# A two-layer block on one core: the loop over further rounds moved ahead of the experts, and the last expert's rows added by one-hot products

## The chip, the cores and the metric

The kernel runs on one core of one Trainium2 chip. A core has five engines with an instruction queue each, worked off in order: TensorE (PE; its weight loads are listed as PEld), VectorE (DVE), ScalarE (ACT), GpSimd (POOL) and SyncE (SP, which here only issues DMAs). The metric is the device time of one execution in microseconds (us), from the first to the last instruction and what lies around them.

## The reference

Two transformer blocks over 1024 rows of width 1024. The change concerns the end of the second one, the mixture of experts, and the last norm:

```python
expert_idx = (g_sel[:, None] * EXPERTS_PER_GROUP + top_i).reshape(-1)   # 2 of 32 experts per row
order = jnp.argsort(expert_idx)
counts = jnp.bincount(expert_idx, length=N_EXPERTS)
...
def expert_block(args):                      # 128 rows of one expert
    xb, e = args
    hb = jax.nn.silu(xb @ w_g[e]) * (xb @ w_u[e])     # 1024 -> 512
    return hb @ w_d[e]                                # 512 -> 1024
...
y = y_pad[dest] * gates[order][:, None]
out = jnp.zeros((t, d), xt.dtype).at[token_idx[order]].add(y)
...
x = x + out
return rms_norm_2(x, norm_final)
```

## The kernel before

All of the work up to the experts (attention layers, norms, the router) is untouched. Then `route` (L1358 on) works out which rows go to which expert, and two products (`table`, L1462) write `idt`: for each of the 32 experts a list of up to 128 row numbers to read (column 0) and up to 128 places in `y_d` to write (column 1; `y_d` in HBM has two rows for each row of x, one for each of its two experts). `rounds_t` says how many further rounds of 128 rows the fullest expert needs.

**The experts.** The work is cut into 192 units (L1536 to 1541): for each expert e two halves of the gate weights (g), two of the up weights (u) and, one expert later, two of the down weights (d). So the order is g(e) g(e) u(e) u(e) d(e-1) d(e-1), and at the very end d(31) d(31). A unit is 1 MB of weights: SP loads it (`eraw`), ACT writes its rounded copy (`ehi`), DVE the remainder (`elo`; POOL does it for the second u unit of each expert, L1579), and PE runs 12 products of 512 columns over it, in threes (`mm3`, L131): high by high, high by low, low by high. Splits run two units ahead of PE (`AHEAD`), with three buffers of `ehi` and `elo`. The ring of loaded weights has 6 slots (11 for the first 150 units). The code is in `tc.manual_schedule()`: every engine runs its instructions in the order in which the loop at L1590 writes them.

**Rows in and out.** `gather` (L1492) is an indirect DMA from POOL's queue that reads an expert's 128 rows into `xe`. PE transposes them (`x_part`). After the second d unit of an expert, `scatter` (L1529) copies the two PSUM banks `yo` to `ys` on ACT, and POOL issues an indirect DMA that writes the 128 rows to their places in `y_d`. Each such write waits for the one before it, since both write `y_d`.

**The further rounds.** Behind the experts stands a loop (L1652) over `rounds`, and in it one over the 32 experts (L1653), that does the same work for rows beyond the first 128. `rounds` is read into a register of every engine at L1651. With these inputs it is zero: the trace has no instruction of the inner loop, but all engines pass the read and the branch.

**The end.** For each of 8 tiles of 128 rows (L1684): load both y rows of every row (`fy`, 1 MB), two DVE instructions that scale and add them to the rows of x (`x3t`, loaded from L1638), a square with sum on ACT, the reciprocal root on POOL (`rsq`, L199), and the final scaling: for even tiles ACT by the root and POOL by the norm's weights, for odd tiles one DVE instruction. Then the tile goes out.

Of the kernel before, what the change touches and what calls it, by code (L numbers as in the profile page):

```python
# [27 lines left out]
def block_kernel(  # L28
# [1505 lines left out]


    units = []  # L1536
    for e in range(NE + 1):
        if e < NE:
            units += [(nm, e, half) for nm in "gu" for half in range(2)]
        if e:  # L1540
            units += [("d", e - 1, half) for half in range(2)]
# [29 lines left out]
    for i in range(len(wide)):  # L1571
        if i not in raws:
            load_unit(i)
    AHEAD = HB - 1
    parts, banks, hbs, hss, tps, xss, yos = {}, {}, {}, {}, {}, {}, {}

    def split_unit(i):
        nm, e, half = units[i]
        parts[i] = esplit(raws.pop(i), pool if (nm, half) == ("u", 1) else dve)  # L1579

    with tc.manual_schedule():
        for e in range(2):
# [7 lines left out]
        for i, (nm, e, half) in enumerate(units):  # L1590
# [44 lines left out]
    x3t = []
    for i in range(4):
        xt = er2.tile([128, 2048], F32, name="x3t", tag="eraw2", bufs=RAWB2)
        sp.dma_start(out=xt.rearrange("p (a n) -> p a n", a=2),  # L1638
                     in_=x3_d[i * 256:(i + 1) * 256, :].rearrange("(a p) n -> p a n", p=128))
        x3t += [xt[:, 0:D], xt[:, D:]]  # L1640
    nfw = er2.tile([128, 2048], F32, name="nfw", tag="eraw2", bufs=RAWB2)[:, 0:D]
    sp.dma_start(out=nfw, in_=norm_final_2.partition_broadcast(128))


    shift = mo.tile([128, 1], F32, name="shift")
    pool.memset(shift, float(C))

    rounds_e = ew.tile([128, D], I32, name="rounds_e", tag="ys", bufs=2)
    dve.tensor_copy(out=rounds_e[:, 0:1], in_=rounds_t)
    with tc.tile_critical():  # L1650
        rounds = nc.values_load(rounds_e[0:1, 0:1], min_val=0, max_val=7)  # L1651
    with tc.For_i(0, rounds) as r_:  # L1652
        with tc.For_i(0, NE) as e_:  # L1653
            pos = ew.tile([128, 16], F32, name="pos", tag="pos", bufs=1)
            TS(pos, posk, shift, SUB)
            ti = ew.tile([128, 2], I32, name="ti", tag="ti", bufs=1)
            table(pos, lambda j: tkr[:, j], 2, ti)
            gather(xes[0], ti[:, 0:1])
            xs = x_tile()
            for g in range(2):  # L1660
                x_part(xes[0], xs, g)
            gu = []
            for w in (w_e_gate_2, w_e_up_2):
                o = bank("gu", 4)
                for half in range(2):
                    up_half(o, xs, esplit(eload(w[bass.ds(e_, 1), half].rearrange("o p n -> (o p) n")), dve), half)
                gu.append(o)
            hb = ew.tile([128, 512], F32, name="hb", tag="hb", bufs=2)
            A(hb, gu[0], AF.Silu)
            TT(hb, hb, gu[1], MUL)  # L1670
            tp = bank("tpe", 2)
            h_part(tp, hb)
            hs = h_tile()
            split(*hs, tp.rearrange("p (k n) -> p k n", k=4))
            yo = y_bank()
            for half in range(2):
                down_half(yo, hs, esplit(eload(w_e_down_2[bass.ds(e_, 1), half].rearrange("o p n -> (o p) n")), dve),
                          half)
            scatter(yo, ti[:, 1:2])
            TS(shift, shift, 1024.0, ADD)  # L1680
        TS(shift, shift, float(C - NE * 1024), ADD)


    for t in range(8):  # L1684
        rs = slice(t * 128, (t + 1) * 128)
        xt = x3t[t]
        yt = er.tile([128, 2 * D], F32, name="fy", tag="eraw", bufs=RAWB)
        sp.dma_start(out=yt, in_=y_d.rearrange("(t k) d -> t (k d)", k=2)[rs, :])
        STT(xt, yt[:, 0:D], pk[:, 0, t:t + 1], xt, MUL, ADD)
        STT(xt, yt[:, D:], pk[:, 1, t:t + 1], xt, MUL, ADD)  # L1690
        r = rstd_of(xt, D, junk_tile())
        if t % 2 == 0:
            A(xt, xt, AF.Copy, scale=r)
            TT(xt, xt, nfw, MUL, eng=pool)
        else:
            STT(xt, xt, r, nfw, MUL, MUL)
        sp.dma_start(out=out[0, rs, :], in_=xt)
# [35 lines left out]
```

## Time and profile before

| | |
|---|---|
| Device time, median of 3 runs | 2148.75 us (2148.54 to 2151.77) |
| Device time of the profiled execution | 2150.52 us |
| Its span, first to last instruction | 2148.8 us |
| Share of the span busy: PE, PEld, DVE, ACT, POOL | 91%, 77%, 67%, 55%, 29% |
| HBM read, written | 356.35 MB, 39.85 MB |

The shares are means over stages that differ. The experts run from about 1471 us to 2089 us; what follows up to 2148.8 us is the loop that is passed and the end. Rows of the profile give a start and a duration, the engine (a small q stands for its instruction sequencer or DMA queue), the line, the operation, out<-in by the names of the program, and in brackets the idle time before and what ended it.

### The profile page before, as it was taken

To read this page: it belongs to the slowest core of one execution; us is meant where nothing else is said; L and a number is where in the kernel's file an instruction comes from. 1 tells how busy PE (TensorE), PEld (TensorE's weight loads), DVE (VectorE), ACT (ScalarE), POOL (GpSimd) and SP (SyncE) were. 2 spreads that over 40 slices of the span, in tenths; PEclk is the share of its full clock that TensorE was granted. 3 is DMA by queue.
4 is the path that set the end of the run, shared out by engine and by line. 5 is a ranking of instruction groups with operands and counts; after the bars stand their busy time and mean duration, and the time that the engine had idled before them with its cause. 6 is when DMAs were issued, how large, how long until landed. Compare 5 with 4: busy or idle time off the path is not lost.

```text
span 2148.8 us, 32901 instructions
## 1 busy us (share of the span) xinstructions
PE 1961.3 (91%) x12914; PEld 1653.1 (77%) x12914; DVE 1446.0 (67%) x1923; ACT 1177.3 (55%) x1868; POOL 632.5 (29%) x522
## 2 busy tenths in 40 slices
PE   3999899999999999999999999995999999999980
PEld 2878796887777988889887997894777777777760
DVE  6476774656687754686557855746777777877765
ACT  3454553445465533564335634643777777777752
POOL 3362110144453000241004300003444444344425
PEclk8999999999997999999999999996999999999995
DMA  9212334621111263212622156464999999999956
GB/s 295 70 50 57 111 90 137 193 78 40 31 40 30 60 191 90 64 45 85 191 59 59 51 161 205 157 245 178 347 366 361 379 355 357 358 360 354 360 202 240
DMA packets 218934, 381.60 MB, mean 178 GB/s; under 512 B 50165, under 2 KB 173077, under 8 KB 193177
## 3 DMA queue, kind: packets, MB, share of 16 engines
q1 hardware_dynamic: 194520, 345.79, 46.9%
q10 hardware_dynamic: 15040, 16.89, 2.3%
q0 software_dynamic: 9216, 16.80, 2.1%
q8 instruction: 102, 1.67, 0.3%
q14 instruction: 56, 0.45, 0.1%
HBM read 356.35 MB, written 39.85 MB: 184 GB/s over the span
## 4 chain that ended last, share of the span: by engine, by line
PE 51%; issue 25%; POOL 9%; DVE 7%; DMA 6%; ACT 3%; POOLq 0%; ACTq 0%; SPq 0%; DVEq 0%; another core or an unknown queue 0%
PE mm L133 11%; PE mm L134 11%; PE mm L135 11%; POOL xe L1493 3%; PE tp L189 3%; POOL y_d L1532 2%; PE z L741 1%; DMA xp<-u_d 1%; PE sc L1139 1%; PE sc L1168 1%; PE at L599 1%; PE at L601 1%; PE os L770 1%; DVE wlo L43 1%; DVE kp L43 1%
## 5 line engine op out<-in xcount | busy, mean ns | idle before, releaser
L43 DVE TENSOR_TENSOR elo<-eraw,ehi 128x2048 fp32r<-128x2048 f32 x160 | 402.0, 2528 | 131.2 <-ACT ehi L40 131.2
L40 ACT ACTIVATE ehi<-eraw 128x2048 fp32r<-128x2048 f32 x192 | 366.9, 1912 | 18.8 <-PE yo L135 12.6
L133 PE MATMUL mm<-whi,fs 128*128 128x256 f32 x1152 | 335.4, 293 | 0.9 <-ACT whi L40 0.9
L134 PE MATMUL mm<-wlo,fs 128*128 128x256 f32 x1152 | 334.4, 291 | 0.8 <-DVE wlo L43 0.8
L135 PE MATMUL mm<-whi,fs 128*128 128x256 f32 x1152 | 331.1, 289 | 0.0
L43 DVE TENSOR_TENSOR wlo<-raw,whi 128x1024 fp32r<-128x1024 f32 x156 | 198.6, 1273 | 148.3 <-ACT whi L40 146.7
L40 ACT ACTIVATE whi<-raw 128x1024 fp32r<-128x1024 f32 x156 | 164.8, 1056 | 214.8 <-PE mm L134 93.9
L133 PEld LDWEIGHTS mm<-whi,fs 128*128 128x128 f32 x1152 | 225.0, 196 | 9.0 <-issue 5.5
L134 PEld LDWEIGHTS mm<-wlo,fs 128*128 128x128 f32 x1152 | 225.6, 196 | 8.1 <-issue 6.0
L135 PEld LDWEIGHTS mm<-whi,fs 128*128 128x128 f32 x1152 | 224.2, 195 | 2.4 <-issue 2.3
L134 PE MATMUL gu<-elo,xh 128*128 128x512 f32 x512 | 207.1, 405 | 15.9 <-POOL elo L43 14.4
L133 PE MATMUL gu<-ehi,xh 128*128 128x512 f32 x512 | 208.0, 406 | 2.5 <-ACT ehi L40 2.5
L133 PE MATMUL mm<-fs,whi 128*128 128x512 f32 x480 | 197.2, 414 | 7.5 <-DVE mst L43 4.1
L135 PE MATMUL gu<-ehi,xl 128*128 128x512 f32 x512 | 202.9, 396 | 0.0
L134 PE MATMUL mm<-fs,whi 128*128 128x512 f32 x480 | 197.0, 410 | 1.2 <-DVE fs L52 1.2
L135 PE MATMUL mm<-fs,wlo 128*128 128x512 f32 x480 | 195.1, 406 | 0.0
L43 POOL TENSOR_TENSOR elo<-eraw,ehi 128x2048 fp32r<-128x2048 f32 x32 | 147.6, 4612 | 97.2 <-ACT ehi L40 97.2
L134 PEld LDWEIGHTS gu<-elo,xh 128*128 128x128 f32 x512 | 96.6, 189 | 47.1 <-POOL elo L43 24.6
L133 PEld LDWEIGHTS mm<-fs,whi 128*128 128x128 f32 x480 | 94.0, 196 | 39.4 <-issue 9.6
L133 PEld LDWEIGHTS gu<-ehi,xh 128*128 128x128 f32 x512 | 96.7, 189 | 23.8 <-ACT ehi L40 2.9
L135 PEld LDWEIGHTS gu<-ehi,xl 128*128 128x128 f32 x512 | 96.5, 189 | 21.5
L135 PEld LDWEIGHTS mm<-fs,wlo 128*128 128x128 f32 x480 | 94.2, 196 | 23.4 <-issue 4.0
(467 smaller groups left out, 4234.5 us busy)
## 6 DMA issues: line engine op xcount, KB each, us to landing
eraw<-in_w_e_up_dram SPq DMA_DIRECT2D x64, 1024.0 KB, 7.1
eraw<-in_w_e_down_dram SPq DMA_DIRECT2D x64, 1024.0 KB, 7.3
eraw<-in_w_e_gate_dram SPq DMA_DIRECT2D x64, 1024.0 KB, 7.6
raw<-in_w_in_dram SPq DMA_DIRECT2D x92, 512.0 KB, 3.8
raw<-in_w_out_dram SPq DMA_DIRECT2D x32, 512.0 KB, 3.5
wa<-in_w_ada_dram SPq DMA_DIRECT2D x16, 512.0 KB, 5.9
fy<-y_d SPq DMA_DIRECT2D x8, 1024.0 KB, 8.7
xt<-in_x_dram SPq DMA_DIRECT2D x8, 512.0 KB, 5.6
```

Of the source, the lines that this page charges most:

```text
L40: act.activation(out=o, in_=i, func=f, **kw)
L43: (eng or dve).tensor_tensor(out=o, in0=a, in1=b, op=op)
L133: pe.matmul(out=o, lhsT=l[0], rhs=r[0], start=start, stop=False)
L134: pe.matmul(out=o, lhsT=l[0], rhs=r[1], start=False, stop=False)
L135: pe.matmul(out=o, lhsT=l[1], rhs=r[0], start=False, stop=stop)
L189: pe.transpose(o[0:s.shape[-1], j * 128:j * 128 + s.shape[0]], s, ident[0:s.shape[0], 0:s.shape[0]])
L599: pe.matmul(out=ov[:, hh, ch], lhsT=full[:, hh, ch], rhs=v(ch, hh), start=True, stop=s0 is None)
L601: pe.matmul(out=ov[:, hh, ch], lhsT=qs[r, ch * 128:(ch + 1) * 128], rhs=s0[r], start=False, stop=True)
L741: pe.matmul(out=zp[:, 0:w], lhsT=qc[r, pr, t * 128:(t + 1) * 128], rhs=kc_full[r, pr, s0 * 128:s0 * 128 + w], start=True, stop=True)
L770: pe.matmul(out=os_[:, hd * 64:hd * 64 + 64], lhsT=pt[:, j * 128:(j + 1) * 128], rhs=vc_full[:, s0 + j, hd * 64:hd * 64 + 64], start=(hd = ...
L1493: pool.indirect_dma_start(out=xe, out_offset=None, in_=xn_d[:, :], in_offset=bass.IndirectOffsetOnAxis(ap=itok, axis=0), bounds_check=S - ...
L1532: pool.indirect_dma_start(out=y_d[:, :], out_offset=bass.IndirectOffsetOnAxis(ap=irow, axis=0), in_=ys, in_offset=None, bounds_check=2 * S ...
```

## The change

Five edits. The loop over further rounds, with its read of `rounds`, now stands between the routing and the experts. The last expert's second g unit and its two u units come after the down units of expert 30, so that the order ends g(31) d(30) d(30) g(31) u(31) u(31) d(31) d(31). Expert 31 writes nothing to `y_d`: its places are written with zeros right after expert 0's rows, and its own rows are multiplied into place from SBUF with one-hot matrices that `last_places` prepares behind d(26). The loads of x and of the norm's weights are issued behind d(27), those of the y rows behind d(30). And the end is spread over ACT (scaling of the second y row), POOL (adding it), PE, DVE and ACT again.

```diff
     def scatter(yo, irow):
...
+        put(ys, irow)
+
+    def put(ys, irow):
         pool.indirect_dma_start(out=y_d[:, :], out_offset=bass.IndirectOffsetOnAxis(ap=irow, axis=0),
                                 in_=ys, in_offset=None, bounds_check=2 * S - 1, oob_is_err=False)
...
+        new = [(nm, e, half) for nm in "gu" for half in range(2)] if e < NE else []
+        old = [("d", e - 1, half) for half in range(2)] if e else []
+        units += new[0:1] + old + new[1:] if e == NE - 1 else new + old
...
+    for e in range(2):
+        gather(xes[e], idt[:, e, 0:1])
...
+    with tc.tile_critical():
+        rounds = nc.values_load(rounds_t[0:1, 0:1], min_val=0, max_val=7)
+    with tc.For_i(0, rounds) as r_:
+        with tc.For_i(0, NE) as e_:
...
+    def last_places():
+        d_ = mo.tile([128, 2, 8], F32, name="d_")
+        TS(d_, posk.rearrange("p (i t) -> p i t", i=2), -1024.0 * (NE - 1), ADD)
+        g_ = mo.tile([128, 2, 8], F32, name="g_")
+        TS(g_, d_, 0.0, ALU.is_ge)
+        TT(g_, g_, pk, MUL)
+        TT(pkl, g_[:, 0], g_[:, 1], ADD)
+        TT(d_[:, 0], d_[:, 0], d_[:, 1], MAX)
+        m = ew.tile([128, 8, 128], F32, name="lm", tag="ys", bufs=2)
+        TT(m, islot[:, None].to_broadcast([128, 8, 128]), d_[:, 0, :, None].to_broadcast([128, 8, 128]), ALU.is_equal)
+        for g in range(2):
+            tp = bank("tpe", 2)
+            transpose4(tp, [m[:, 4 * g + i] for i in range(4)])
+            A(onehot[:, 4 * g:4 * g + 4], tp.rearrange("p (k n) -> p k n", k=4), AF.Copy)
...
+    def first_sum(t):
+        yt, xt = yts[t], x3t[t]
+        A(yt[:, D:], yt[:, D:], AF.Copy, scale=pk[:, 1, t:t + 1])
+        STT(xt, yt[:, 0:D], pk[:, 0, t:t + 1], xt, MUL, ADD)
+        TT(xt, xt, yt[:, D:], ADD, eng=pool)
+        if len(yts) < 8:
+            row_of_y()
+
+    def last_sum(t, ys):
+        xt = x3t[t]
+        for n in range(2):
+            o = bank("gu", 4)
+            for i, p_ in enumerate(ys):
+                pe.matmul(out=o, lhsT=onehot[:, t], rhs=p_[:, n * 512:n * 512 + 512], start=(i == 0), stop=(i == 1))
+            STT(xt[:, n * 512:n * 512 + 512], o, pkl[:, t:t + 1], xt[:, n * 512:n * 512 + 512], MUL, ADD)
+        A(junk_tile(), xt, AF.Square, scale=float(D) ** -0.5, accum_out=ssf[:, t:t + 1])
+
+    def last_norm(t0, t1):
+        rsq(ssf[:, t0:t1], ssf[:, t0:t1], t1 - t0)
+        for t in range(t0, t1):
+            STT(x3t[t], x3t[t], ssf[:, t:t + 1], nfw_[0], MUL, MUL)
+            sp.dma_start(out=out[0, t * 128:(t + 1) * 128, :], in_=x3t[t])
...
-                if half:
+                if half and e < NE - 1:
                     scatter(yos.pop(e), idt[:, e, 1:2])
+                    if e == 0:
+                        zt = ew.tile([128, D], F32, name="zt", tag="ys", bufs=2)
+                        pool.memset(zt, 0.0)
+                        put(zt, idt[:, NE - 1, 1:2])
+                    if e == NE - 6:
+                        last_places()
+                    if e == NE - 5:
+                        rest_of_stream()
+                    if e == NE - 2:
+                        rows_of_y()
...
+        ys = [ew.tile([128, 2048], F32R, name="e" + p_, tag="e" + p_, bufs=HB)[:, 0:D] for p_ in ("hi", "lo")]
+        yo = yos.pop(NE - 1).rearrange("p a n -> p (a n)")
+        for t in range(2):
+            first_sum(t)
+        split(*ys, yo)
+        for t in range(2, 4):
+            first_sum(t)
+        for t in range(4):
+            last_sum(t, ys)
+            first_sum(4 + t)
+        last_norm(0, 4)
+        for t in range(4, 8):
+            last_sum(t, ys)
+            if t % 2:
+                last_norm(t - 1, t + 1)
```

`rest_of_stream` issues the four loads of `x3t` (1 MB each) and that of the norm's weights (0.5 MB), `rows_of_y` the first six loads of `fy`; the other two follow when a slot comes free.

Three places in the order of instructions matter below. The first is ACT between the routing and the experts. `idt` is the table that the first gather reads. Before, it is followed at once by the copies of the first expert's rows:

```order
L40 ACTIVATE gd<-gd 128x32 [waits DVE_49]
L40 ACTIVATE d<-d 128x8 [waits DVE_49]
L40 ACTIVATE idt<-gu,twos 128x64 [waits PE_49,Pool_49]
L40 ACTIVATE xh<-tpe 128x512 [waits PE_49] x2
L40 ACTIVATE ehi<-eraw 128x2048 [waits DMAHW1_49,Activation_49]
```

Now it stands behind the read of `rounds` (L1593) and in front of the branch past the loop (L1594), with a wait for SP that was not there:

```order
L40 ACTIVATE gd<-gd 128x32 [waits DVE_49]
L40 ACTIVATE d<-d 128x8 [waits DVE_49]
L1808 UNCONDITIONAL_BRANCH [waits DMAHW2_49,DMAHW1_49,DMAHW3_49,DMAHW0_49,DMAHW4_49,SP_sequencer_49,DMAHW5_49,DVE_49,DMAHW6_49,PE_49,DMAHW7_49,Activation_49,Pool_49]
L1593 TENSOR_LOAD rounds_t
L1592 UNCONDITIONAL_BRANCH
L40 ACTIVATE idt<-gu,twos 128x64 [waits SP_49,PE_49,Pool_49]
L1594 COMPARE_AND_BRANCH
```

The read and the branch have moved in between. The second place is POOL around expert 0's write to `y_d` (`y_d<-ys`). DMASWn is the semaphore of POOL's n-th DMA lane of eight, taken in turn. Before:

```order
L1493 DMA xe_14940<-xn_d,idt 128x1024 [waits DMASW1_49,PE_49]
L43 TENSOR_TENSOR elo<-eraw_14858,ehi 128x2048 [waits DMAHW4_49,Activation_49]
L1493 DMA xe_14939<-xn_d,idt 128x1024 [waits DMASW2_49,PE_49]
L1532 DMA y_d<-ys,idt 2048x1024 [waits Activation_49]
L43 TENSOR_TENSOR elo<-eraw,ehi 128x2048 [waits DMAHW4_49,Activation_49]
```

Now the zeros (`zt`) and their write stand between it and POOL's next split:

```order
L43 TENSOR_TENSOR elo<-eraw_14858,ehi 128x2048 [waits Activation_49]
L1493 DMA xe_14939<-xn_d,idt 128x1024 [waits DMASW4_49,PE_49]
L1535 DMA y_d<-ys,idt 2048x1024 [waits Activation_49]
L1750 MEMSET zt 128x1024
L1535 DMA y_d<-zt,idt 2048x1024 [waits DMASW7_49,Pool_49]
L43 TENSOR_TENSOR elo<-eraw,ehi 128x2048 [waits DMAHW2_49,Activation_49]
L1493 DMA xe_14940<-xn_d,idt 128x1024 [waits DMASW5_49,PE_49]
```

The new write has a wait on lane 7. The third place is DVE behind the second d unit of expert 26. Before, one remainder follows the other:

```order
L43 TENSOR_TENSOR xl_19014<-tpe_19041,xh_19013 128x512 [waits Activation_49]
L43 TENSOR_TENSOR elo_19054<-eraw_18974,ehi_19053 128x2048 [waits DMAHW2_49,Activation_49]
L43 TENSOR_TENSOR elo_19073<-eraw_18994,ehi_19072 128x2048 [waits DMAHW3_49,Activation_49]
L43 TENSOR_TENSOR elo_19096<-eraw_19022,ehi_19095 128x2048 [waits DMAHW4_49,PE_49,Activation_49]
L43 TENSOR_TENSOR hl_19118<-tpe_19106,hh_19117 128x512 [waits Activation_49]
```

Now the six instructions of `last_places` stand between the second and the third; `lm` is what PE transposes:

```order
L43 TENSOR_TENSOR elo_19280<-eraw_19200,ehi_19279 128x2048 [waits DMAHW3_49,Activation_49]
L43 TENSOR_TENSOR elo_19299<-eraw_19220,ehi_19298 128x2048 [waits DMAHW4_49,Activation_49]
L47 TENSOR_SCALAR d__19319<-posk_14841 128x16
L47 TENSOR_SCALAR g__19321<-d__19319 128x16 [waits DVE_49]
L43 TENSOR_TENSOR g__19321<-g__19321,pk_14842 128x16 [waits DVE_49]
L43 TENSOR_TENSOR pkl_15230<-g__19321 128x8 [waits DVE_49]
L43 TENSOR_TENSOR d__19319<-d__19319 128x8
L43 TENSOR_TENSOR lm_19326<-islot_14844,d__19319 128x1024 [waits DMASW6_49,DMASW7_49,DMASW2_49,DVE_49]
L43 TENSOR_TENSOR elo_19343<-eraw_19248,ehi_19342 128x2048 [waits DMAHW5_49,PE_49,Activation_49]
```

On PE the eight transposes of `lm` follow directly on the last product of d(26), ahead of the next g unit.

## Rows read from the trace of the kernel before

**Rows 1.** Busy us per engine (instructions) in stretches; then PE clock, DMA share, GB/s
```profile
1560.00:1700.00 140.00, 136.52 (x626) 108.95 (x625) 109.21 (x67) 105.05 (x82) 60.68 (x22) 1.00 0.96 366
2089.30:2148.80 59.50, 0.00 (x0) 0.00 (x0) 31.08 (x20) 14.33 (x21) 28.06 (x21) 0.53 0.55 217
```

**Rows 2.** Chain that ended last, 2088 to 2112 us: start, us, what
```profile
2089.25 1.03 ACT ys L40
...
2091.39 5.22 POOLq L1650
...
2097.49 3.43 DMA y_d<-ys,idt
...
2101.72 4.80 DMA fy<-y_d
```

**Rows 3.** Timeline of the end: start, us, engine, line, operation, form [idle before]
```profile
2114.12 3.36 DVE L52 SCALAR_TENSOR_TENSOR x3t<-fy,pk,x3t 128x1024 f32<-128x1024 f32 x1
...
2140.34 1.04 ACT L40 ACTIVATE junk<-x3t 128x1024 bf16<-128x1024 f32 x1
2140.51 2.34 POOL L43 TENSOR_TENSOR x3t<-x3t,nfw 128x1024 f32<-128x1024 f32 x1 [1.26 <-ACT x3t L40]
...
2143.85 1.28 DVE L52 SCALAR_TENSOR_TENSOR x3t<-x3t,rstd,nfw 128x1024 f32<-128x1024 f32 x1 [5.01 <-POOL rstd L43]
```

**Rows 4.** Timeline between routing and experts: the table's last products, the first gather
```profile
1468.67 1.68 PE L1470 MATMUL gu<-rr,mt__14954 128*128 128x64 f32 x7
...
1471.65 1.31 POOL L1493 DMA_INDIRECT xe<-xn_d,idt  x1 [9.01 <-issue]
```

**Rows 5.** L1729, POOL's drains: count, shortest/median/longest ns, first and last start
```profile
L1729 POOLq DRAIN  x3: 51/110/769, 2143.2 to 2148.5; - x3
```

**Rows 6.** Timeline behind expert 0's last unit: POOL, DVE, PE
```profile
1518.38 1.16 POOL L1532 DMA_INDIRECT y_d<-ys,idt  x1 [4.45 <-ACT ys L40]
...
1522.14 0.68 DVE L43 TENSOR_TENSOR hl<-tpe,hh 128x512 fp32r<-128x512 f32 x1
1522.32 4.62 POOL L43 TENSOR_TENSOR elo<-eraw,ehi 128x2048 fp32r<-128x2048 f32 x1 [2.78 <-ACT ehi L40]
...
1526.99 0.50 PE L134 MATMUL gu<-elo,xh 128*128 128x512 f32 x1 [0.43 <-POOL elo L43]
```

**Rows 7.** DMA issues, 1518 to 1519 us: queue, operation, us from issue to landing
```profile
y_d<-ys,idt POOLq DMA_INDIRECT x1, 8.1
```

**Rows 8.** Timeline behind d(26): DVE, ACT, PE
```profile
2003.79 4.48 DVE L43 TENSOR_TENSOR elo<-eraw,ehi 128x2048 fp32r<-128x2048 f32 x2
...
2006.70 1.03 ACT L40 ACTIVATE ys<-yo 128x1024 f32<-128x1024 f32 x1 [0.89 <-PE yo L135]
...
2007.91 0.60 PE L189 MATMUL tpe<-ident,hb 128*128 128x128 f32 x4
```

**Rows 9.** Timeline of the routing, DVE: the shapes that `last_places` has
```profile
1466.43 1.22 DVE L43 TENSOR_TENSOR mt__14954<-islot,pos 128x1024 fp32r<-128x1024 f32 x1
...
1468.90 0.15 DVE L47 TENSOR_SCALAR mc<-mc 128x1 f32<-128x1 f32 x1
```

**Rows 10.** DMA issues: the fifth fy load (2103.77 us); all loads of down weights
```profile
fy<-y_d SPq DMA_DIRECT2D x1, 1024.0 KB, 12.7
...
eraw<-in_w_e_down_dram SPq DMA_DIRECT2D x64, 1024.0 KB, 7.3
```

**Rows 11.** Timeline: the load of one d(28) unit, and ACT's copy of it
```profile
2021.52 0.33 SPq L1482 DMA_DIRECT2D eraw<-in_w_e_down_dram  x1
...
2035.30 1.91 ACT L40 ACTIVATE ehi<-eraw 128x2048 fp32r<-128x2048 f32 x1
```

**Rows 12.** Timeline of the last expert: end of d(29), DVE's hl, first product of d(31)
```profile
2063.14 1.03 ACT L40 ACTIVATE ys<-yo 128x1024 f32<-128x1024 f32 x1 [0.88 <-PE yo L135]
...
2068.20 0.68 DVE L43 TENSOR_TENSOR hl<-tpe,hh 128x512 fp32r<-128x512 f32 x1
...
2083.10 0.51 PE L133 MATMUL yo<-ehi,hh 128*128 128x512 f32 x1 [1.16 <-ACT hh L40]
```

More of the change, by code (lines that the diff above doesn't have):

```diff
@@ L1573, in block_kernel, with lsplit @@
             load_unit(i)
+    for e in range(2):
+        gather(xes[e], idt[:, e, 0:1])
+    def lsplit(src):
+        raw = ew.tile([128, 2048], F32, name="lraw", tag="elo", bufs=HB)
+        sp.dma_start(out=raw, in_=src)
+        hi = ew.tile([128, 2048], F32R, name="lhi", tag="ehi", bufs=HB)
+        lo = ew.tile([128, 2048], F32R, name="llo", tag="elo", bufs=HB)
+        split(hi, lo, raw)
+        return hi, lo
+    shift = mo.tile([128, 1], F32, name="shift")
+    pool.memset(shift, float(C))
+    with tc.tile_critical():
+        rounds = nc.values_load(rounds_t[0:1, 0:1], min_val=0, max_val=7)
+    with tc.For_i(0, rounds) as r_:
+        with tc.For_i(0, NE) as e_:
+            pos = ew.tile([128, 16], F32, name="pos", tag="pos", bufs=1)
+            TS(pos, posk, shift, SUB)
+            ti = ew.tile([128, 2], I32, name="ti", tag="ti", bufs=1)
+            table(pos, lambda j: tkr[:, j], 2, ti)
+            lx = ew.tile([128, D], F32, name="lx", tag="ys", bufs=2)
+            pool.memset(lx, 0.0)
+            gather(lx, ti[:, 0:1])
+            xs = x_tile()
+            for g in range(2):
+                x_part(lx, xs, g)
+            gu = []
+            for w in (w_e_gate_2, w_e_up_2):
+                o = bank("gu", 4)
+                for half in range(2):
+                    up_half(o, xs, lsplit(w[bass.ds(e_, 1), half].rearrange("o p n -> (o p) n")), half)
+                gu.append(o)
+            hb = ew.tile([128, 512], F32, name="hb", tag="hb", bufs=2)
+            A(hb, gu[0], AF.Silu)
+            TT(hb, hb, gu[1], MUL)
+            tp = bank("tpe", 2)
+            h_part(tp, hb)
+            hs = h_tile()
+            split(*hs, tp.rearrange("p (k n) -> p k n", k=4))
+            yo = y_bank()
+            for half in range(2):
+                down_half(yo, hs, lsplit(w_e_down_2[bass.ds(e_, 1), half].rearrange("o p n -> (o p) n")), half)
+            scatter(yo, ti[:, 1:2])
+            TS(shift, shift, 1024.0, ADD)
+        TS(shift, shift, float(C - NE * 1024), ADD)
     AHEAD = HB - 1
@@ L1579, in split_unit @@
         parts[i] = esplit(raws.pop(i), pool if (nm, half) == ("u", 1) else dve)
+    onehot = mo.tile([128, 8, 128], F32R, name="onehot")
+    pkl = mo.tile([128, 8], F32, name="pkl")
+    def last_places():
[8 more added lines that the diff above has]
+        TT(m, islot[:, None].to_broadcast([128, 8, 128]), d_[:, 0, :, None].to_broadcast([128, 8, 128]), ALU.is_equal)
+        for g in range(2):
+            tp = bank("tpe", 2)
+            transpose4(tp, [m[:, 4 * g + i] for i in range(4)])
+            A(onehot[:, 4 * g:4 * g + 4], tp.rearrange("p (k n) -> p k n", k=4), AF.Copy)
@@ new lines, in block_kernel, with rest_of_stream @@
+    x3t, yts, nfw_ = [], [], []
+    def rest_of_stream():
+        for i in range(4):
+            xt = er2.tile([128, 2048], F32, name="x3t", tag="eraw2", bufs=RAWB2)
+            sp.dma_start(out=xt.rearrange("p (a n) -> p a n", a=2),
+                         in_=x3_d[i * 256:(i + 1) * 256, :].rearrange("(a p) n -> p a n", p=128))
+            x3t.extend((xt[:, 0:D], xt[:, D:]))
+        nfw_.append(er2.tile([128, 2048], F32, name="nfw", tag="eraw2", bufs=RAWB2)[:, 0:D])
+        sp.dma_start(out=nfw_[0], in_=norm_final_2.partition_broadcast(128))
@@ new lines, in row_of_y, with rows_of_y @@
+    def row_of_y():
+        t = len(yts)
+        yt = er.tile([128, 2 * D], F32, name="fy", tag="eraw", bufs=RAWB)
+        sp.dma_start(out=yt, in_=y_d.rearrange("(t k) d -> t (k d)", k=2)[t * 128:(t + 1) * 128, :])
+        yts.append(yt)
+    def rows_of_y():
+        for _ in range(RAWB):
+            row_of_y()
+    ssf = mo.tile([128, 8], F32, name="ssf")
+    def first_sum(t):
[4 more added lines that the diff above has]
+        if len(yts) < 8:
+            row_of_y()
@@ L1581, in block_kernel @@
     with tc.manual_schedule():
-        for e in range(2):
-            gather(xes[e], idt[:, e, 0:1])
         xss[0] = x_tile()
@@ L1632, in block_kernel @@
                     load_unit(k)
[L1635 to L1642, printed above, removed]
@@ L1645, in block_kernel @@
[L1645 to L1681, printed above, removed]
@@ L1684, in block_kernel @@
[L1684 to L1697, printed above, removed]
+        ys = [ew.tile([128, 2048], F32R, name="e" + p_, tag="e" + p_, bufs=HB)[:, 0:D] for p_ in ("hi", "lo")]
```

5 lines of the change are left out of this document (1 added, 4 removed).

## Prediction

> **What bounds the kernel now.** I read the page's busy shares first, then a table by stretches, then the chain of waits, then timelines at each place that the change touches. In the middle of the expert stage PE is busy 136.5 of 140 us [rows 1]: PE sets the time there, 18.84 us for an expert (603 us from 1471 to 2089, by 32). DMA is nearly full as well, 0.96, so there is little room to catch up on loads. Whatever makes PE stand still in this stage lengthens the span by as much, unless it falls into a gap that is there already. From 2089.3 us on PE does nothing for 59.5 us. The chain [rows 2] shows its beginning: the copy `ys` of expert 31, POOL's drain at the loop (5.22), the write of expert 31's rows (issued at 2097.49, landed 3.43 later), the first `fy` load (issued at 2101.72, 4.80 to land). Then come eight tiles of sums and norms until DVE's last instruction ends at 2143.85 + 1.28 = 2145.13 [rows 3]; the out DMA and the end take 3.7 more. I call 2089.2, the end of the last product, T0. The end costs 59.6 us behind it.
>
> So the change trades two things: less behind T0, and more instructions in a stage that PE bounds. I work out five costs (a to e) and one gain (f).
>
> **a. The loop ahead of the experts.** `idt` is written by ACT behind the read of `rounds`, and POOL's first gather stands behind the branch. Today the table's product ends at 1468.67 + 1.68 = 1470.35 and the gather starts at 1471.65 [rows 4]. What is added is read from the loop of before [rows 2]: from the end of `ys` (2090.28) to the start of the drain 1.1 (read and barrier), the drain itself, and from the landing of the write (2100.92) to the next issue 0.8 (branch and hand-over), so 1.9 plus the drain. The drain is the unknown. At the loop it took 5.22, right behind the experts' last work; POOL's other drains took 0.05 to 0.77 [rows 5]. By the nearer case, an idle POOL, I take 0.4. Sum 2.3, bounds 1.9 and 7.1. Nothing covers it, since PE has nothing to do before the first rows. The weight loads are issued ahead of it and are not later, so no more than this is lost.
>
> **b. The zeros behind expert 0's rows.** The write of the zeros goes to the same `y_d`, so it waits on POOL for expert 0's write to land. That was issued at 1518.38 [rows 6] and took 8.1 us to land [rows 7], to 1526.5. The zeros' own issue takes 1.16 like the one before it, to 1527.7. Queued behind it on POOL is the split `elo` of the second u unit, 4.62: it ends at 1532.3, where it ended at 1526.94 before, and PE's next product waited for exactly that instruction even then (0.43 idle, [rows 6]). Nothing else is ready for PE ahead of it. Cost 5.4. Were the write to land in 3.43 as at the end [rows 2], it would be 0.7; a little more than 5.4 is possible through the gather behind it: bounds 0.7 and 6.5. I take 5.4, because the 8.1 is this very write.
>
> **c. The one-hot matrices behind d(26).** PE's eight transposes wait for `lm` on DVE. `ys` starts at 2006.70 [rows 8], so d(26) ends at about 2006.6. DVE's two splits run to 2003.79 + 4.48 = 2008.27. Behind them come five small instructions; one of 128x1 takes 0.15 [rows 9], with 16 columns and a hand-over 0.2 each is my estimate, 1.0; and `lm`, of the shape of `mt` but not rounded, 1.22 [rows 9]. So `lm` ends at 2010.5 and PE stood still for 3.8. Eight transposes are two times 0.60 [rows 8]: 1.2. DVE is late by 2.2 for its next split, mostly inside that gap. 5.0 and some 0.4 for hand-overs make 5.4. Were a good part hidden by what PE already does in the order, only the transposes would remain, 1.2; with the splits late in addition it is 7. I take 5.4.
>
> **d. 4.5 MB in front of the weights.** Loads run through one queue at the rate of the `fy` loads: the fifth was issued at 2103.77 and landed 12.7 later [rows 10], 2116.47, the first at 2106.52 [rows 2], so four took 9.95, 2.49 us each. `x3t` and the norm's weights are 4.5 of these, 11.2 us of delay for the weights behind. How early are those? The load of a d(28) unit goes out at 2021.52 and is copied at 2035.30 [rows 11], a lead of 13.8 against 7.3 to land [rows 10]: 6.5 to spare. 11.2 - 6.5 = 4.7 if nothing else gives, 0 if most units are loaded further ahead than this one. I take the middle, 2.5, bounds 0 and 5.
>
> **e. The new order of the last expert.** With P for the end of d(29), 2063.1 [rows 12], the last product of before ends at P + 26.0. Now one g unit (to P + 3.4) is followed by d(30), which needs expert 30's `hl` (2068.20 + 0.68, P + 5.7, [rows 12]) sooner than its other units would have: a stop of 1.8. d(30) ends at P + 10.85. The u units come next, and the second has its remainder from POOL (4.62) behind POOL's write: ready at P + 18.5 where PE wants it at P + 16.7, another 1.8. After that `hb` and d(31)'s remainder stand behind each other on DVE, which has to take turns with POOL's split (as in f); my estimate from these is that d(31) starts near P + 24.9 and takes 6.1. Before, its first product came at 2083.10, P + 20.0. The end is at P + 31.0: cost 5.0, bounds 3 and 6.
>
> Costs: 2.3 + 5.4 + 5.4 + 2.5 + 5.0 = 20.6.
>
> **f. The end.** The write of expert 30 goes out some 19 us before the last product, so `fy` lands early, tiles 2.5 us apart, and the first two tiles are summed under d(31). From the new last product T on, ACT has the rounded copy of `yo` (1.1), DVE its remainder (to 2.4), then ACT scales and each tile needs a DVE sum and a POOL sum. How these two go together decides. A DVE sum of two SBUF sources takes 1.28 alone but 3.36 while POOL works at a product of the same kind, and POOL's takes 2.34 [rows 3]. The 3.36 is the rest of POOL's instruction and then its own time: they take turns. So each tile costs 1.2 + 2.3 = 3.5: from 4.95 (tile 2's sum on DVE done) POOL is through with tile 2 at 7.2, tile 6 at 21.2, tile 7 at 23.5. The placed halves have one source in PSUM. `hl`, of that kind, took its usual 0.68 with POOL's split starting in it [rows 6], so I let them (0.69 each) run beside POOL. Then the root on POOL, 1.0 (between the end of POOL's instruction at 2142.85 and DVE's at 2143.85, [rows 3]), four norms of 1.28 to 29.6. The tiles 4 to 7 come in two pairs, each two placed tiles of 1.4, the square (1.04, [rows 3]) with the root 1.0 and hand-overs, 2.2, two norms of 1.28: 7.6 a pair, to 44.8, and 3.7 to the end: 48.5. That is 11.1 less than 59.6. If DVE and POOL don't take turns, the sums are through 5.6 earlier: 42.9, a gain of 16.7. If the placed halves take turns too, eight of them fall between POOL's sums, 5.4 more: 53.9, a gain of 5.7.
>
> A rule bears on this. In the Trainium skill, "SBUF — State Buffer", section "Who interferes with whom", a DVE instruction with two SBUF inputs contends with a GpSimd instruction that reads SBUF, and the second to issue is fully blocked, while one with at most one SBUF input is not. It speaks against giving sums to DVE and POOL at once; the trace agrees in the 3.36 against 1.28. By it the end is 48.5; without its exception for a single SBUF input it would be 53.9.
>
> **The sum.** 20.6 - 11.1 = +9.5 on a span of 2148.8: 2158.3. The profiled execution took 2150.52, 1.7 over its span and 1.8 above the median of 2148.75, so against the median it is 2158.2; I say 2158.
>
> **Rivals.** *Larger loss:* the drain costs 5.2 again (+4.8), or the placed halves take turns with POOL (+5.4), or both; 2163 to 2168. For it: the only drain seen at this loop. Against: POOL is idle where the loop stands now.
> *No difference:* the stalls b to e overlap. DMA, at 0.96, gains lead in every stop of PE, so the stop at d(26) would pay for d, and the transposes may find `lm` ready; with c at 1.2, d at 0 and e at 3 the costs are 11.9 and the gain 11.1: about 2149.5.
> *Faster:* DVE and POOL work side by side at the end, 42.9, so 16.7 is gained. This decides as soon as the costs in the stage stay under 16.7. With the write of expert 0 landing as the unloaded one does (b 0.7) and no drain (a 1.9), the costs are 15.5 at my other terms (2147.5), and 8.8 with d at 0 and c at 1.2 also: 2140.9. Against it: the 3.36.
>
> **Chances.** The forecast (+4.3 to +14) 0.54, the larger loss 0.18, no difference 0.15, faster 0.13. A change under 0.2%, 4.3 us, can't be told from none by a measurement of this kernel. So faster 0.13, same 0.15, slower 0.72. The range from 2147 to 2168 leaves out most of the faster case and the far end of the larger loss; the forecast's own is 2153 to 2163.
>
> **What would show it.** a: the first gather 2.3 us later than 1471.65, and no long drain. b: a wait of 4 to 8 us on POOL ahead of the zeros' write, and PE idle for 5 to 6 at the product that reads POOL's `elo` of expert 2. c: PE idle some 4 behind d(26), released by `lm`. d: ACT's `ehi` of an expert 28 or 29 unit waiting for its load. e: two stops of PE under 2 us and a longer wait ahead of d(31). f: an end of about 48, with DVE's sums near 3.5 wherever POOL's run. The forecast is wrong if PE passes b and c without those gaps, or if the end is below 43.

## The result, and the profile after

The changed kernel takes 2166.16 us (median of 4 runs, 2161.28 to 2168.39), the kernel before 2148.64 (4 runs, 2147.08 to 2151.77); the ratio is 1.0091, 95% interval 1.0069 to 1.0113. So it is slower by 17.5 us (the medians) to 19.6 us (the ratio) where 9.5 was forecast: the sign was right, the size about half of what came.

The profiled execution took 2161.28 us, its span is 2159.5. Its work ahead of the routing, which the change does not touch, happens to be 10.5 us shorter than in the profiled execution of before (the table's last product ends at 1459.88 and not at 1470.35). So I count from the table's end: 678.5 us to the last instruction before, 699.7 after, 21.2 more. Below, hb(e) is the start of ACT's activation of expert e's gate, ys(e) the start of its copy behind expert e's down units, T the end of the last product of d(31); each number is a difference of two such starts in one trace.

| stretch, us | before | after | difference | forecast |
|---|---|---|---|---|
| table's end to hb(0) | 20.04 | 23.81 | +3.8 | a: +2.3 |
| hb(2) to hb(3) | 18.84 | 27.88 | +9.0 | b: +5.4 |
| ys(26) to ys(27) | 18.82 | 26.17 | +7.4 | c: +5.4 |
| ys(27) to ys(28) | 18.83 | 25.04 | +6.2 | d: +2.5 |
| ys(29) to T | 26.08 | 33.75 | +7.7 | e: +5.0 |
| T to the last instruction | 59.59 | 48.05 | -11.5 | f: -11.1 |
| all other stretches | 516.26 | 514.97 | -1.3 | 0 |

Of the last line 1.2 lies between hb(3) and ys(26), the undisturbed middle, where the forecast had nothing. The loop alone does not have it, the other runs below do, and none takes it apart.

The middle of the stage and the end, by stretches (busy us of PE, PEld, DVE, ACT, POOL, then PE clock, DMA share, GB/s), beside [rows 1]:

```profile
1560.00:1700.00 140.00, 136.44 (x625) 109.39 (x624) 109.74 (x66) 106.80 (x83) 60.97 (x22) 1.00 0.97 367
2111.50:2159.50 48.00, 13.78 (x32) 7.81 (x32) 31.99 (x31) 16.45 (x23) 22.00 (x12) 0.58 0.31 121
```

PE is as busy in the middle as before. The stops are at the five places that the forecast names. At the head (ACT and POOL, beside [rows 4]; POOL's drain ahead of `idt`, at 1461.06, took 0.05, not the 5.22 of [rows 2]):

```profile
1461.20 0.31 ACT L40 ACTIVATE idt<-gu,twos 128x64 int32<-128x64 f32 x1 [11.40 <-SPq L1592]
...
1464.07 1.31 POOL L1493 DMA_INDIRECT xe<-xn_d,idt  x1 [11.89 <-issue]
```

Behind expert 0's last unit (POOL, then PE, beside [rows 6]):

```profile
1511.62 1.19 POOL L1535 DMA_INDIRECT y_d<-ys,idt  x1 [4.42 <-ACT ys L40]
...
1521.32 0.99 POOL L1535 DMA_INDIRECT y_d<-zt,idt  x1 [7.54 <-DMA y_d<-ys,idt]
1522.33 4.50 POOL L43 TENSOR_TENSOR elo<-eraw,ehi 128x2048 fp32r<-128x2048 f32 x1
...
1526.89 0.80 PE L134 MATMUL gu<-elo,xh 128*128 128x512 f32 x1 [7.12 <-POOL elo L43]
...
1529.19 0.63 PE L133 MATMUL gu<-ehi,xh 128*128 128x512 f32 x1
```

The zeros wait for expert 0's write (7.54), the split stands behind them, and PE waits 7.12 where it waited 0.43. Then look at the last row: the product that takes 0.39 in the middle of the stage takes 0.63, and its like start 0.43 apart, not 0.23. The same is seen in the granted clock of the stretches around the stops b, c, d and e:

```profile
1515.00:1520.00 5.00, 4.77 (x23) 3.63 (x21) 2.30 (x3) 3.29 (x4) 0.00 (x0) 1.00 1.00 364
1520.00:1525.00 5.00, 0.00 (x0) 0.00 (x0) 4.67 (x3) 1.96 (x2) 3.66 (x2) 0.69 0.71 242
1525.00:1530.00 5.00, 3.11 (x7) 2.48 (x8) 3.99 (x1) 0.00 (x0) 1.83 (x1) 0.50 0.67 224
...
2010.00:2015.00 5.00, 3.45 (x12) 3.09 (x13) 1.37 (x3) 2.07 (x3) 0.24 (x1) 0.51 0.98 399
2015.00:2020.00 5.00, 5.00 (x21) 4.13 (x20) 2.89 (x2) 3.15 (x3) 0.00 (x0) 0.81 0.33 101
...
2050.00:2055.00 5.00, 0.83 (x2) 0.53 (x3) 2.69 (x2) 4.31 (x3) 0.00 (x0) 0.94 1.00 424
2055.00:2060.00 5.00, 5.00 (x17) 3.93 (x17) 5.00 (x4) 2.95 (x3) 0.00 (x0) 0.72 1.01 423
2100.00:2105.00 5.00, 2.83 (x9) 2.17 (x10) 3.62 (x5) 2.67 (x3) 0.18 (x1) 0.72 1.00 423
2105.00:2110.00 5.00, 5.00 (x15) 3.86 (x15) 0.88 (x1) 0.00 (x0) 5.00 (x2) 0.60 1.01 424
```

While PE stands the clock falls from 1.00 to 0.50, that is from 2.4 to 1.2 GHz, and PE then works at half speed for some us: 15 products fill 2105 to 2110, where 23 fitted into 4.77 us from 1515 on. The Trainium skill says so too: by "TensorE: Matmul & The Clock Gate", section "Part 1: The HAM clock gate", the default is the lower of two levels and activity releases it. That rule was not weighed in the forecast.

The other stops, in order: DVE's `lm` and PE behind d(26) ([rows 8]); ACT waiting for a d(28) load ([rows 11]); and the last expert's three waits, on `hl`, on POOL's `elo`, and on `hb` behind two remainders on DVE ([rows 12]):

```profile
2010.18 1.22 DVE L43 TENSOR_TENSOR lm<-islot,d__19319 128x1024 f32<-128x1024 f32 x1
2011.55 1.94 PE L189 MATMUL tpe<-ident,lm 128*128 128x128 f32 x8 [3.84 <-DVE lm L43]
...
2050.37 1.91 ACT L40 ACTIVATE ehi<-eraw 128x2048 fp32r<-128x2048 f32 x1 [6.61 <-DMA eraw<-in_w_e_down_dram]
2052.34 0.49 PE L133 MATMUL yo<-ehi,hh 128*128 128x512 f32 x1 [2.49 <-ACT ehi L40]
2054.66 0.79 PE L134 MATMUL yo<-elo,hh 128*128 128x512 f32 x1 [1.83 <-DVE elo L43]
...
2083.55 0.50 PE L135 MATMUL yo<-ehi,hl 128*128 128x512 f32 x1 [1.72 <-DVE hl L43]
2094.20 6.62 DVE L43 TENSOR_TENSOR elo<-eraw,ehi 128x2048 fp32r<-128x2048 f32 x2 [3.78 <-ACT ehi L40]
2096.53 0.50 PE L134 MATMUL gu<-elo,xh 128*128 128x512 f32 x1 [1.77 <-POOL elo L43]
2101.48 0.66 PE L189 MATMUL tpe<-ident,hb 128*128 128x128 f32 x4 [2.13 <-DVE hb L43]
2102.83 0.80 PE L133 MATMUL yo<-ehi,hh 128*128 128x512 f32 x1 [0.69 <-ACT hh L40]
```

In the end, DVE's sum of two SBUF sources and POOL's take turns, as in [rows 3], while the placed halves (source in PSUM, two in 1.40) run beside POOL:

```profile
2119.50 1.40 DVE L52 SCALAR_TENSOR_TENSOR x3t<-gu,pkl,x3t 128x512 f32<-128x512 f32 x2
2120.82 2.07 DVE L52 SCALAR_TENSOR_TENSOR x3t<-fy,pk,x3t 128x1024 f32<-128x1024 f32 x1
2121.77 12.24 POOL L43 TENSOR_TENSOR x3t<-x3t,fy 128x1024 f32<-128x1024 f32 x4
...
2135.51 4.87 DVE L52 SCALAR_TENSOR_TENSOR x3t<-x3t,ssf,nfw 128x1024 f32<-128x1024 f32 x4 [5.98 <-POOL ssf L43]
```

POOL's four take 3.06 each where one alone takes 2.34, DVE's one 2.07 for 1.28. The first norm starts 24.0 behind T (forecast 24.5).

### The profile page after: what moved, and what is told of

It reads as the page before. It is cut to its first block, busy times and chain, and to the rows that moved or that the text cites. A ratio compares the mean times of both kernels' runs of the same rounds, so it can differ in the third digit from the quotient of the medians.

```text
span 2159.5 us, 32974 instructions
## 1 busy us (share of the span) xinstructions
PE 1969.6 (91%) x12954; PEld 1656.8 (77%) x12954; DVE 1455.6 (67%) x1941; ACT 1183.5 (55%) x1875; POOL 632.6 (29%) x517
## 5 line engine op out<-in xcount | busy, mean ns | idle before, releaser
L43 DVE TENSOR_TENSOR elo<-eraw,ehi 128x2048 fp32r<-128x2048 f32 x160 | 407.0, 2559 | 146.4 <-ACT ehi L40 146.4
```

The lines of the kernel that those rows point to most:

```text
L43: (eng or dve).tensor_tensor(out=o, in0=a, in1=b, op=op)
```

## The experiments

Two theories stood against each other for the 13 us that the stage lost beyond the forecast. One: the five stops are separate, each costs its own wait and, where it is long, a stretch at half clock behind it. The other: one stop makes loads and splits late for the next, and the excess is that lateness. The table has the stretches of every run, measured as above; "end" is T to the last instruction, "total" from the table's end.

| us | to hb(0) | hb(2)-hb(3) | ys(26)-ys(27) | ys(27)-ys(28) | ys(29)-T | end | total |
|---|---|---|---|---|---|---|---|
| before | 20.04 | 18.84 | 18.82 | 18.83 | 26.08 | 59.59 | 678.5 |
| after | 23.81 | 27.88 | 26.17 | 25.04 | 33.75 | 48.05 | 699.7 |
| zeros first | 24.05 | 18.77 | 25.26 | 26.38 | 31.44 | 48.05 | 689.4 |
| one-hot first | 22.91 | 27.02 | 18.78 | 25.89 | 33.74 | 48.06 | 692.0 |
| x loads late | 23.18 | 27.19 | 25.24 | 18.80 | 33.68 | 48.06 | 691.2 |
| order as before | 23.25 | 27.33 | 25.27 | 24.62 | 26.05 | 54.57 | 696.1 |
| PE kept busy | 23.04 | 25.17 | 24.19 | 24.62 | 31.20 | 48.05 | 691.3 |
| sums on DVE | 23.25 | 27.36 | 25.25 | 24.87 | 32.32 | 47.98 | 696.0 |
| loop alone | 23.72 | 18.82 | 18.82 | 18.81 | 26.07 | 52.83 | 675.3 |
| three undone | 23.95 | 18.77 | 18.79 | 18.78 | 34.11 | 48.08 | 677.5 |
| last expert | 24.07 | 18.78 | 18.78 | 18.79 | 26.12 | 52.46 | 674.0 |
| best | 24.05 | 18.77 | 18.79 | 18.78 | 26.13 | 46.60 | 668.2 |

Each row is one profiled execution. Stretches without a stop repeat within 0.1 us (but for ys(28) to ys(29), right behind d, which took 18.8, and 19.20 and 19.33 with the zeros first and with the one-hot matrices first). Stretches with a stop differ from run to run: 27.02 to 27.88 for b, 25.24 to 26.17 for c, 24.62 to 26.38 for d, 31.44 to 34.11 for e in its new order and without added products. The way to hb(0), with the loop ahead of it, takes 22.91 to 24.07. What these differences go with is shown under "PE kept busy".

**Zeros first.**

```diff
         gather(xes[0], idt[:, 2, 0:1])
+        zt = ew.tile(...); pool.memset(zt, 0.0); put(zt, idt[:, NE - 1, 1:2])
...
-                    if e == 0: (the same three)
```

> The zeros for expert 31's places are written right after the first gathers, ahead of every expert, instead of behind expert 0's rows. Theory (the write waits on POOL for expert 0's write to land, and POOL's split stands behind it): the stop of PE ahead of the second u unit of expert 2 (6.8 us) goes, and with it the stretch at half clock behind it; from the first expert to the middle of the stage the kernel is 9.0 us shorter than the changed one, about 2152 to 2155 in all. Rival (the prediction's size of this step, 5.4, the rest belonging to a slower start): only 5 to 6 shorter. Second rival (expert 0's own write now waits as long for the zeros to land, and POOL's split behind it): under 2.

The whole 9.0 went (27.88 to 18.77). Both rivals fall: expert 0's own write does not suffer, since the zeros, issued at 1480.65, landed 9.9 later, long before it went out at 1519.21. The device time, 2158.30, is above the 2152 to 2155 expected, because the work ahead of the routing ended 7.4 later than in the profile of after; from the table's end 10.3 us went.

**One-hot matrices first.**

```diff
     with tc.manual_schedule():
+        last_places()
...
-                    if e == NE - 6:
-                        last_places()
```

> The one-hot matrices are made ahead of the first expert, while the first gather is under way, instead of behind d(26). Theory: the stop behind d(26) and its half clock go, 7.4 us between d(26) and d(28), and the head of the stage gets longer by under 1 us, since PE waits there for the gather anyway (4.5 us). Rival: the lost 7.4 is mostly the weights' loads being late behind d(26), then under 3 come back.

The 7.4 went, and the head did not get longer (22.91; the others that have the loop there take 23.04 to 24.07). The stop d stayed (25.89): it is not c's lateness handed on. There is a little in the forecast's rival that loads gain lead in a stop: PE's wait for the load at d is 1.93 to 2.49 in the runs that have both b and c ahead of it, 2.52 here and 3.02 with the zeros first. That is 1.1 at most.

**Loads of x late.**

```diff
-                    if e == NE - 5:
-                        rest_of_stream()
...
+            if (nm, e, half) == ("d", NE - 2, 0):
+                rest_of_stream()
```

> The loads of x and of the norm's weights (4.5 MB) are issued behind the last weight load instead of behind d(27). Theory: PE's two stops in the second half of d(28) (2.5 and 1.8 us, then a stretch at reduced clock) go, 5.0 us; the y rows still land in time, so the end stays at 48 us. Rival: the stops belong to the one behind d(26), whose lateness passes to the loads; then they stay. Second rival: the y rows come behind x and the end grows by 3 or more.

Here 6.2 went (25.04 to 18.80), with the end unchanged. So d is these loads alone. The 5.0 in the expectation was read from single products; by the `ys` rows the stop is 6.2.

**Order as before.**

```diff
-        units += new[0:1] + old + new[1:] if e == NE - 1 else new + old
+        units += new + old
```

> The last expert's units stand again in the order g g u u d(30) d(30) d(31) d(31); all else is as in the changed kernel. Theory: the last product comes 26 us after d(29) again instead of 34.8, so 8.8 less, of which 2 to 3 is clock; but expert 30's rows are written some 10 us later against the last product, so the y rows come about 5 us behind it and the first two tiles are not summed ahead: the end takes 48 + 8 to 10 = 56 to 58. In all within 2 us of the changed kernel. Rival: the order itself is the loss and the y rows matter little: 5 or more faster.

The product stage got back 7.7 and the end lost 6.5, from 48.05 to 54.57. The total is 3.6 lower, 2.4 of which is the scatter of the head, b, c and d; 1.2 is the order's own. Moving d(30) ahead gained nothing. DVE shows what the end waits for:

```profile
2112.27 1.28 DVE L52 SCALAR_TENSOR_TENSOR x3t<-fy,pk,x3t 128x1024 f32<-128x1024 f32 x1 [7.14 <-DMA fy<-y_d]
```

**PE kept busy.**

```diff
+    def keep_busy(n, e):
+        t = bank("tpe", 2)
+        for _ in range(n):
+            pe.matmul(out=t, lhsT=xss[e][0][:, 0], rhs=xss[e][0][:, 0:4], start=True, stop=True)
...
+                if (nm, e, half) == ("u", 2, 1):
+                    keep_busy(26, 2)
...
                     if e == NE - 6:
+                        keep_busy(20, NE - 5)
                         last_places()
...
                 if e == NE - 1 and half == 0:
+                    keep_busy(8, NE - 1)
```

> The changed kernel, with products that nothing reads (a 512-column product of the rows of x with themselves into a spare bank) put on PE in three of its stops: 26 ahead of the second u unit of expert 2, 20 ahead of the transposes behind d(26), 8 ahead of the last expert's transposes. Each fills most of a wait and delays nothing else by over 1 us. Theory (each stop costs its wait and then some 2 us more, because the granted clock stands at half behind it): the granted clock behind these places stays near 1.0; ys(2) to ys(3) falls from 27.9 to about 25.6, ys(26) to ys(27) from 26.2 to about 24.2, d(31) from 8.7 to about 6.3. Rival (the excess comes from splits and loads that are late behind the stop): the times stay within 0.5 of what they were, or grow by the products.

(The first stretch meant there is that from hb(2) to hb(3), 27.9.) This is the run that tells the theories apart. The waits are about as long as before: from the start of the last instruction ahead of the stop to the one that waited, without the added products, 7.3, 4.8 and 2.5 us, for 7.6, 4.2 and 2.5 in after. But PE has something to do in them, and the granted clock stays up (stretches around b and c, columns as above; then the first product of d(31), beside that of after at 2102.83):

```profile
1517.50:1522.50 5.00, 5.00 (x23) 4.13 (x22) 4.66 (x3) 2.13 (x2) 4.34 (x2) 1.00 0.75 213
1522.50:1527.50 5.00, 4.13 (x20) 3.08 (x20) 4.24 (x2) 0.00 (x0) 1.71 (x1) 1.00 0.79 273
2004.00:2009.00 5.00, 5.00 (x28) 4.23 (x27) 2.27 (x7) 1.26 (x3) 1.18 (x1) 1.00 1.01 387
2009.00:2014.00 5.00, 5.00 (x26) 4.05 (x24) 2.89 (x2) 4.03 (x3) 0.60 (x1) 1.00 0.45 166
...
2095.45 0.50 PE L133 MATMUL yo<-ehi,hh 128*128 128x512 f32 x1 [0.69 <-ACT hh L40]
```

With 54 additional products the kernel is faster: b by 1.9 to 2.7, c by 1.1 to 2.0 against the runs that have these stops without them, and ys(29) to T by 2.5 against after. That last one is nearly within the scatter of its stretch (31.44 with the zeros first), but d(31) by itself, from its first product to T, takes 6.12 for 8.66. Where no products were put, at d, nothing changed (24.62). The rival predicted no change or a loss.

The scatter of the table says the same without any added product. Each stretch with the mean clock that was granted in it:

| us, clock | hb(2)-hb(3) | ys(26)-ys(27) | ys(29)-T |
|---|---|---|---|
| after | 27.88, 0.82 | 26.17, 0.87 | 33.75, 0.90 |
| x loads late | 27.19, 0.87 | 25.24, 0.93 | 33.68, 0.90 |
| sums on DVE | 27.36, 0.88 | 25.25, 0.93 | 32.32, 0.95 |
| PE kept busy | 25.17, 1.00 | 24.19, 1.00 | 31.20, 1.00 |

With the zeros first (ys(29) to T 31.44, clock 0.95) the low clock came ahead of the wait for `hb`, which shrank from 2.13 to 0.78, and d(31) ran in 6.13. The head is no other case: its first product starts 13.0 to 13.4 behind the table's end wherever the loop stands there, and from that product to hb(0) it takes 10.65 at a clock of 0.63 (after), 10.06 at 0.70 (x loads late) and 9.75 at 0.73 (PE kept busy). So the same stop costs more or less as the clock comes back later or sooner. The clock behind a stop is shown as a cost of its own.

**Sums on DVE.**

```diff
-        A(yt[:, D:], yt[:, D:], AF.Copy, scale=pk[:, 1, t:t + 1])
         STT(xt, yt[:, 0:D], pk[:, 0, t:t + 1], xt, MUL, ADD)
-        TT(xt, xt, yt[:, D:], ADD, eng=pool)
+        STT(xt, yt[:, D:], pk[:, 1, t:t + 1], xt, MUL, ADD)
```

> In the end, the second y row of each tile is scaled and added by one DVE instruction (1.22 alone), as the first one is, instead of by ACT and POOL. Theory (a POOL and a DVE instruction of two SBUF sources take turns, so that POOL's sum takes time from DVE): the end does not get longer though DVE has 8 instructions more; 46 to 47 instead of 48.05. Rival (they work side by side, and DVE sets the end): longer by 6 x 1.22 = 7.3, so 55.

47.98 against 48.05. DVE took over eight more instructions of 1.28 and the end did not move, which excludes the rival (55); but the gain of 1 to 2 did not come either. Two engines that take turns are worth one here, and not less.

**The loop alone** (the kernel before, with the loop and the two gathers moved as in the change, and no other edit).

> The kernel before, with the loop over further rounds moved ahead of the experts and nothing else. Theory: the head of the expert stage gets 3.8 longer (from the table's end to the first hb, 20.0 to 23.8, as in the changed kernel), no other stage changes up to the last product, and the end loses the drain of 5.2, the register read and the branch, 1.9 together: 59.6 to about 52.5. In all 3.3 faster from the table's end on. Rival (a drain of that length must be paid for wherever the read stands): the head is 7 or more longer.

Head +3.7, end -6.8, total -3.1: as expected, and no other stretch moves. The expected -3.3 is met within 0.2. So 6.8 of the 11.5 that the changed kernel gains at the end is the loop's.

**Three undone** (the first three edits together).

> Zeros first, one-hot matrices first and the late loads of x together. Theory (three separate stops, which add up): from the table's end to the end 699.7 - 9.1 - 7.4 - 6.2 = 677, against 678.5 of the kernel before: no difference left. Rival (they share a cause, a queue that is late): 5 or more away from that.

677.5 for 677 expected: the three stops are separate, and they add up. What remains of the change costs as much as it gives. Beside the loop alone (675.3) it is 2.2 slower: the last expert's new path gains 4.8 more at the end (48.08 for 52.83) and loses 8.0 ahead of it (34.11 for 26.07).

**The last expert**, on top of these.

```diff
-        units += new[0:1] + old + new[1:] if e == NE - 1 else new + old
+        units += new[0:2] + old + new[2:] if e == NE - 1 else new + old
...
-        parts[i] = esplit(raws.pop(i), pool if (nm, half) == ("u", 1) else dve)
+        parts[i] = esplit(raws.pop(i), pool if (nm, half) == ("u", 1) and e < NE - 1 else dve)
...
+            late_split = (nm, e, half) == ("u", NE - 1, 1)
-            if i + AHEAD < len(units):
+            if i + AHEAD < len(units) and not late_split:
...
                         TT(hbs[e], hbs[e], banks.pop(("u", e)), MUL)
+                        if late_split:
+                            split_unit(i + AHEAD)
```

> The three undone edits again, and in the last expert: order g g d(30) d(30) u u d(31) d(31), DVE instead of POOL for the remainder of its second u unit, and the remainder of the last d unit behind the product of gate and up on DVE. Theory (expert 31's stops are POOL's split behind its DMA issue, hl behind a remainder, and hb behind a remainder on DVE): from ys(29) to the last product 27.6 instead of 34.1, which is 1.5 over the kernel before; the end stays near 48 as long as the y rows land in time. From the table's end on 671. Rival (the loss belongs to the half clock behind the wait for hb, which stays): over 31.

The stops of the last expert are named rightly: ys(29) to T fell to 26.12, even below the 27.6 expected. But the end grew to 52.46 where 48 was expected: T now comes before most of the y rows do. DVE's first sum starts 0.5 ahead of T (2081.50), its second waits for its load until 2083.99, and the split of the last expert's rows, behind both, starts 4.3 behind T (1.2 in after).

**Best.**

```diff
-            (the order of first_sum, last_sum and last_norm at the end of the kernel)
+        for t in range(3):
+            first_sum(t)
+        split(*ys, yo)
+        for t in range(3, 8):
+            first_sum(t)
+        for t in range(8):
+            last_sum(t, ys)
+        last_norm(0, 4)
+        last_norm(4, 8)
```

> The last one, and in the end: both y rows summed on DVE, three tiles ahead of the last expert's split instead of two, all placed rows ahead of all norms, so that the roots are worked out beside other work. Theory (DVE's own time is what the end costs): 2.4 for the split, 12.5 for five sums, 11 for the placed halves, 9.8 for the norms, 3.7 to finish: 40 instead of 48. From the table's end on 663 against 678.5 of the kernel before, a ratio of about 0.993. Rival (the y rows are late, since the last product now comes earlier): the end is 45 or more.

2133.98 us, ratio 0.9944 to the kernel before, interval 0.9923 to 0.9964 (medians of 6 and of 11 runs): faster than the kernel before, by 0.6%, and by the stretches 31.5 us shorter than the changed one. The end is 46.60 and so the rival's case; the expected 40 failed on the y rows. The write of expert 30 goes out at 2076.84, while x is still being loaded. SP waits for it to land and issues the first `fy` load at 2084.47, 7.6 later (3.5 in after, where x had landed long before), and DVE waits 5.44 for that load until 2090.05, T itself:

```profile
2076.84 0.99 POOL L1535 DMA_INDIRECT y_d<-ys,idt  x1 [10.45 <-ACT ys L40]
...
2084.47 11.05 SPq L1667 DMA_DIRECT2D fy<-y_d  x8
...
2090.05 7.64 DVE L52 SCALAR_TENSOR_TENSOR x3t<-fy,pk,x3t 128x1024 f32<-128x1024 f32 x6 [5.44 <-DMA fy<-y_d]
```

## Why the prediction was wrong

- **f, the end, was right**: 48.5 forecast, 48.05 measured, by the mechanism forecast (turns for two SBUF sources, none for the placed halves). The pieces came as forecast too: the first norm 24.0 behind T for 24.5, a pair of the last tiles 7.5 for 7.6. The rule of the Trainium skill that it quotes holds on both sides: 2.07 for 1.28, and 1.40 for two placed halves beside a busy POOL.
- **a was right that there is no long drain (0.05, 0.4 was taken), somewhat low in the rest**: 3.8 for 2.3. The gather comes 2.9 later against the table's end and the first product 2.8; the other 1.0 lies between that product and hb(0) (10.65 for 9.70), where the clock was 0.63 and before 0.73.
- **b failed in size**: the step "Cost 5.4" had the right chain, but priced PE's wait alone. The wait is longer (the zeros are issued 9.7 behind expert 0's write, 8.1 was taken), and behind it PE works at half clock: 9.0 in all, 6.3 with the clock held.
- **c failed in the same step**: the wait was 3.84 (3.8 forecast). What the forecast lacks is the half clock: the eight transposes took 1.94 for 1.2, and the products behind them 0.63 for 0.39. With the clock held the stretch is 5.4 longer than before, the 5.4 that was forecast.
- **d failed in the choice between its bounds**: the working gave 4.7, and "I take the middle, 2.5" threw half of it away for cover that no row showed. The two waits are 2.49 + 1.83 = 4.3; of the rest of the 6.2 some 1.4 is the clock, an estimate from the row of 2055 to 2060 (5 us of a busy PE at 0.72), which no run here took apart.
- **e had the right waits, and again no clock**: 7.7 for 5.0. PE waits 1.7 and 1.8, as forecast, and then 2.1 on `hb`; d(31) starts 25.1 behind d(29), where 24.9 was forecast. The failure is "takes 6.1": d(31) took 8.66, and 6.12 with the clock held, where the stretch is 5.1 longer than before. The wait on `hb` has a cause that the forecast listed as an item and not as the point of the edit: before, d(30) stood between expert 31's up units and its down units and covered `hb` (the wait on `hh` was there before too, 1.16 for 0.69 now). Moved ahead, it covers it no more.
- **The rivals.** "Larger loss" held the right time (2163 to 2168) with the wrong reason: neither the long drain nor turns for the placed halves. So it is luck that 2166 lies in the range of 2147 to 2168 given under the chances; the forecast's own ended at 2163. "The stalls overlap" is refuted, since three undone edits add up to 22.2 us for 9.0 + 7.4 + 6.2 = 22.6.
- **A slip without effect:** the 18.84 us for an expert is right by the stretches (18.79 to 18.84 each), but "603 us from 1471 to 2089" is 32 times 18.84; those two times are 618 apart, with the head and the last expert's tail in them.

So the failed step is one that stands ahead of the terms, "Whatever makes PE stand still in this stage lengthens the span by as much": a stop was priced as long as it lasts, and the half clock behind it at nothing. The run with PE kept busy shows the half clock at b, c and d(31) as 7.2 us against after (2.7 + 2.0 + 2.5), of the 13.4 that the five terms lacked; at full clock the forecast's c and e are right to 0.1. The rest is d (3.7, some 1.4 of it clock), a (1.5, 1.0 of it in the stretch at a lower clock) and the longer wait of b (6.3 - 5.4 = 0.9).

## What to carry to other kernels

A stop of a busy PE can cost more than its wait, since the products behind it may run at half speed: look at the granted clock in the stretch behind a gap of like length. Here it fell at every wait of 3.8 or 7 us that was left empty; behind the waits of 1.7 to 1.8 at the end of the stage it fell in some runs and not in others. Before work is put ahead of a bound engine's next instruction, look for a place where that engine waits anyway: the zeros and the one-hot matrices cost 16 us where they were written and at most 0.4 ahead of the first expert, where the first product starts 13.0 to 13.4 behind the table's end with or without them. And when a block of work is moved earlier, ask what it covered where it stood.

## What the runs showed of the hardware

- Useless products made the kernel faster: 54 of them, in waits of about the same length, kept the granted clock at 1.00 at the three places where they were put.
- The same stop did not cost the same twice: 25.24 to 26.17 for the stretch with c, as the mean granted clock in it was 0.93 or 0.87, and 24.19 at 1.00.
- The same indirect write landed in 3.43 us at a quiet end [rows 2] and in the loaded stage 9.7 us passed from its issue to that of the zeros, which wait for it; in the best kernel 7.6 passed from its issue to that of the load that waits for it (2076.84 to 2084.47) while x was being loaded.
- A drain at a register read took 0.05 with POOL idle, and 5.22 behind the experts.
- The stages ahead of the routing, the same in every kernel, ended anywhere from 1458 to 1470 us. A change of 10 us can't be read from two spans, but it can from stretches that start at the same instruction.
